# Two blocks of fp32 layers on one core: four weight buffers of each kind, gated products ended token tile by token tile, later transposes in the feed-forwards

## The chip, the cores and the metric

One core of a Trainium2 chip runs the whole program. The metric is device time in microseconds (us), the median of several executions. The core has a matrix engine (TensorE, PE in the rows), a vector engine (VectorE, DVE), a scalar engine (ScalarE, ACT), GpSimd (POOL) and a queue engine (SyncE, SP) that here only issues transfers.

## The reference

The first block has two layers of feed-forward, mixer, feed-forward. The second has an even layer (Hyena convolution with window attention, then an MLP, both for 256 tokens and 256 context tokens) and an odd one (retention, then an MLP for the tokens alone), each modulated by rows that come from a small conditioning product (ada). Width is 1024, batch 1, all in fp32.

```python
x = x + 0.5 * swiglu(rms_norm(x), w_gate, w_up, w_down)       # 2816 wide
x = x + merged @ w_out                                        # mixer
x = x + 0.5 * swiglu(rms_norm(x), ...)
...
x = x + g_a * y_l                                             # even, odd mixer
x = x + g_m * sq_relu_mlp(modulate(rms_norm_2(x)), w1, w2)    # 4096 wide
ctx = ctx + cg_a * y_c
ctx = ctx + cg_m * sq_relu_mlp(modulate(rms_norm_2(ctx)), w1, w2)
...
return rms_norm_2(x, final_g)
```

## The kernel before, in words

Each fp32 product is made of three matmuls on split operands: high by high, high by low and low by high. Weights come in tiles of two k tiles by 512 columns (512 KB). `wload` (L237) issues the transfer into wraw on SP, rounds it to whi on ScalarE (L251) and subtracts to get wlo on VectorE (L252). A short table, `ENG`, sets for the first tiles after a gated output product which subtraction goes to POOL instead (one after a product of two token tiles, two after one of four). Buffers of wraw, whi and wlo are 4, 3 and 3, taken in turn in `wtile`; the feed-forwards add 3, 1 and 1 and the mixers of the first block 0, 1 and 1.

`gemm` (L261) keeps a token tile of 128 still and moves 512 weight columns through, for 2 or 4 token tiles (L291 to L293). It takes the weight tiles in order; for the last group, if `skew` says so, it takes each token tile to its end before the next. `gemm_t` (L299) keeps weights still and moves tokens (L333 to L335), 256 or 512 columns.

`ffn` (L456) walks the 2816 columns in six chunks. Each chunk is a gate product, an up product, av (L473, VectorE), eight transposes of av on TensorE (L477), and their split into ahi and alo (L480); then `residual` (L445) does the down product. `out_gated` (L1323) is the output product of both mixers of the second block and of the MLPs: when a token tile ends, `add_gated` (L1053, L1054) adds it to x or ctx, and the norm of the next stage begins: `prep_mod` (L399) transposes x (L410), takes row statistics (L353, L359, L343, POOL for the power, L345), spreads the scales with a ones product (L424 from junk, L423; rb, L425), and then scales (L429) and splits (hA L432, hB L433) the operand of the next stage. Between them are three handovers: even mixer to MLP 0, MLP 0 to odd mixer, odd mixer to MLP 1. In the first block kdup (L565) is an operand of the mixer's attention, transposed at L670.

A tile scheduler sets the order on each engine from the program's order and its priorities; ada work (L987, L999, L1003) is put in between as background, a step per weight load. Each engine takes its instructions strictly in that order. The token-tile end reads

```python
elif last:
    order = [(k, t) for t in range(nt) for k in part]
```

Of the kernel before, what the change touches and what calls it, by code (L numbers as in the profile page):

```python
# [11 lines left out]
F32 = mybir.dt.float32  # L12
# [20 lines left out]

ENG = {2: [0, 1], 4: [0, 1, 1]}
# [65 lines left out]
class Net:  # L100
# [30 lines left out]
    def setup(self):  # L131
# [3 lines left out]
        self.eng = []  # L135
# [90 lines left out]
    def wtile(self, name, shape):  # L226

        own = {"wraw": 4, "whi": 3, "wlo": 3}[name]
# [8 lines left out]
    def wload(self, src, k0, nk, c0, cn):  # L237
# [8 lines left out]
        with self.tc.high_priority(120 if self.loads <= 2 else 0):  # L246
            e = self.eng.pop(0) if self.eng else 0
            if e & 2:
                nc.gpsimd.tensor_copy(hi[sl], raw[sl])
            else:  # L250
                nc.scalar.copy(hi[sl], raw[sl])  # L251
            (nc.gpsimd if e & 1 else nc.vector).tensor_sub(lo[sl], raw[sl], hi[sl].bitcast(F32))  # L252
# [8 lines left out]
    def gemm(self, lhs, nk, src, c0, cn, nt, k_base=0, mid=None, done=None, skew=(False, False), turn=0):  # L261
# [7 lines left out]
        group = 2 if cn > 256 else 1  # L269
        i = 0  # L270
        while i < len(plan):
            if mid and i == min(2, len(plan) - 1):
                mid()
            n = 1
            if nt == 4 and i == 0 and skew[0] or skew[1] and i == len(plan) - group:
                n = group
# [5 lines left out]
            if i == 0 and skew[0] and nt == 4:  # L282
                order = [(k, t) for ts in ((0, 1), (2, 3)) for k in part for t in ts]
# [4 lines left out]
            for (kt, wh, wl), t in order:  # L288
                h, l = lhs(kt + k_base, t)
# [9 lines left out]
    def gemm_t(self, hT, nk, src, c0, cn, tok, skew=False, whole=False):  # L299
# [10 lines left out]
        group = 2 if cn > 256 else 1  # L310
        i = 0
        while i < len(plan):
# [86 lines left out]
    def prep_mod(self, x, m, tok, kind, xA):  # L399

        nc = self.nc
        ss = self.sm.tile([128, 2, 4], F32, name="ssm")
        seen = []

        def piece(c0, cn):
            k0 = c0 // 128
            ps = [self.tp.tile([128, 2, 256], F32, name="tp") for _ in range(cn // 256)]
            for t in range(2):
                for i in range(cn // 128):
                    nc.tensor.transpose(ps[i // 2][:, i % 2, t * 128:t * 128 + 128], x[:, t, (k0 + i) * 128:(k0 + i) * 128 + 128], self.ident)  # L410
            for i in range(cn // 128):
                nc.scalar.activation(xA[:, k0 + i], ps[i // 2][:, i % 2], AF.Copy, scale=m[:, tok, kind + 1, k0 + i:k0 + i + 1])
            self.row_stats(x, ss, len(seen), c0=c0, cn=cn)
            seen.append(c0)

        rb = self.act.tile([128, 1, 256], F32, name="rb", bufs=2)
# [1206 lines left out]
```

## Time and profile before

| what | value |
|---|---|
| median of 3 runs | 2446.25 us (2445.13 to 2447.65) |
| profiled execution, its own time | 2448.74 us |
| its span | 2447.0 us |
| TensorE busy | 2379.9 us (97%) |
| VectorE busy | 1542.1 us (63%) |
| ScalarE, POOL busy | 1107.5 us (45%), 145.1 us (6%) |
| DMA | 405.85 MB, 166 GB/s mean |

The span is the profiled part of one execution; the rest of the execution's own time lies around it. Matmuls overlap, so a busy TensorE is not one at its peak. PEclk in a window is the clock granted to TensorE, 1.00 for the full one. A wait is put down to what ended it last.

### The profile page before, as it was taken

How to read it: one execution, taken by the hardware profiler on the slowest of the kernel's cores; microseconds unless marked ns; L12 is line 12 of the kernel's file. 1: busy time of each engine (PE TensorE's matmuls, PEld its weight loads, DVE VectorE, ACT ScalarE, POOL GpSimd, SP SyncE). 2: the span in 40 equal slices, each digit the busy share in tenths (PEclk: the TensorE clock that was granted, in tenths of full speed). 3: DMA queues.
4: the chain of work that ended last, by engine and by line, in shares of the span. 5: the costliest groups of instructions: out<-in, count | busy, mean ns of one | idle time of the engine just before them, and what ended most of it. 6: DMA issues, size and time to landing. Idle time of an engine off the chain costs nothing. (4 is left out here: it accounts for less than half of the span.)

```text
span 2447.0 us, 31298 instructions
## 1 busy us (share of the span) xinstructions
PE 2379.9 (97%) x11941; PEld 1924.1 (79%) x11941; DVE 1542.1 (63%) x2237; ACT 1107.5 (45%) x1715; POOL 145.1 (6%) x175
## 2 busy tenths in 40 slices
PE   9999999999999999999999999999999999999998
PEld 7887777778788867778887767788887888887996
DVE  5775677756767557685855765555534654565665
ACT  5444664544444456554543434331424433334543
POOL 2000100110000000000000001000001110110000
PEclk9999999999999999999999999999999999999999
DMA  8775536856777554586642122645432433344664
GB/s 273 249 254 183 165 121 196 265 168 211 241 215 225 174 164 140 163 277 186 218 146 90 53 86 69 193 167 170 141 99 86 140 103 104 112 129 138 198 182 137
DMA packets 212350, 405.85 MB, mean 166 GB/s; under 512 B 14830, under 2 KB 48365, under 8 KB 211688
## 3 DMA queue, kind: packets, MB, share of 16 engines
q1 hardware_dynamic: 207416, 391.77, 50.8%
q0 software_dynamic: 3776, 9.38, 1.2%
q10 hardware_dynamic: 1008, 2.70, 0.3%
q8 instruction: 94, 1.54, 0.3%
q14 instruction: 56, 0.46, 0.1%
HBM read 401.48 MB, written 4.67 MB: 166 GB/s over the span
## 5 line engine op out<-in xcount | busy, mean ns | idle before, releaser
L252 DVE TENSOR_TENSOR wlo<-wraw,whi 128x1024 fp32r<-128x1024 f32 (+1 forms) x617 | 750.8, 1221 | 588.1 <-ACT whi L251 585.9
L251 ACT CAST whi<-wraw 128x1024 fp32r<-128x1024 f32 (+1 forms) x622 | 649.1, 1046 | 952.5 <-PE acc L293 707.7
L291 PE MATMUL acc<-whi,hA 128*128 128x512 f32 (+1 forms) x1472 | 561.0, 381 | 1.8 <-ACT hA L378 0.8
L292 PE MATMUL acc<-wlo,hA 128*128 128x512 f32 (+1 forms) x1472 | 556.9, 378 | 0.3 <-DVE wlo L252 0.3
L293 PE MATMUL acc<-whi,hA 128*128 128x512 f32 (+2 forms) x1152 | 432.5, 375 | 1.4 <-DVE hA L379 1.4
L291 PEld LDWEIGHTS acc<-whi,hA 128*128 128x128 f32 x1472 | 278.1, 189 | 61.0 <-issue 8.6
L292 PEld LDWEIGHTS acc<-wlo,hA 128*128 128x128 f32 x1472 | 278.3, 189 | 49.1 <-DVE wlo L252 1.7
L291 PE MATMUL acc<-whi,ahi 128*128 128x512 f32 x736 | 288.5, 392 | 0.0
L293 PE MATMUL acc<-whi,alo 128*128 128x512 f32 x736 | 286.8, 390 | 0.0
L292 PE MATMUL acc<-wlo,ahi 128*128 128x512 f32 x736 | 286.7, 390 | 0.0
L333 PE MATMUL acc<-hA,whi 128*128 128x512 f32 (+1 forms) x752 | 259.5, 345 | 6.4 <-ACT rl L1385 3.4
L334 PE MATMUL acc<-hA,wlo 128*128 128x512 f32 (+1 forms) x752 | 259.2, 345 | 2.4 <-POOL wlo L252 2.4
L335 PE MATMUL acc<-hB,whi 128*128 128x512 f32 (+1 forms) x752 | 257.8, 344 | 0.0
L293 PEld LDWEIGHTS acc<-whi,hA 128*128 128x128 f32 x1152 | 218.0, 189 | 40.4 <-DVE hA L379 2.0
L333 PEld LDWEIGHTS acc<-hA,whi 128*128 128x128 f32 x752 | 144.8, 193 | 25.2 <-ACT rl L1385 3.8
L291 PEld LDWEIGHTS acc<-whi,ahi 128*128 128x128 f32 x736 | 138.2, 188 | 30.2 <-issue 2.3
L334 PEld LDWEIGHTS acc<-hA,wlo 128*128 128x128 f32 x752 | 145.1, 193 | 21.4 <-issue 3.4
L293 PEld LDWEIGHTS acc<-whi,alo 128*128 128x128 f32 x736 | 138.2, 188 | 29.3 <-issue 0.4
L292 PEld LDWEIGHTS acc<-wlo,ahi 128*128 128x128 f32 x736 | 138.2, 188 | 28.1 <-issue 0.2
L335 PEld LDWEIGHTS acc<-hB,whi 128*128 128x128 f32 x752 | 144.6, 193 | 17.2 <-issue 1.4
L999 DVE SCALAR_TENSOR_TENSOR hB<-hB,cT 128x1024 f32<-128x1024 f32 x112 | 141.0, 1279 | 22.1 <-DMA hB<-in_ada_w_dram 21.8
L293 PE MATMUL acc<-whi,hB 128*128 128x512 f32 (+1 forms) x320 | 121.5, 382 | 2.5 <-DVE hB L433 2.4
(422 smaller groups left out, 2544.2 us busy)
## 6 DMA issues: line engine op xcount, KB each, us to landing
wraw<-in_mlp_w_dram SPq DMA_DIRECT2D x128, 512.0 KB, 3.8
wraw<-in_ffn_w_gate_dram SPq DMA_DIRECT2D x88, 512.0 KB, 4.2
wraw<-in_ffn_w_up_dram SPq DMA_DIRECT2D x88, 512.0 KB, 4.6
wraw<-in_ffn_w_down_dram SPq DMA_DIRECT2D x88, 512.0 KB, 4.0
wraw<-in_w_in_dram SPq DMA_DIRECT2D x84, 512.0 KB, 3.7
hB<-in_ada_w_dram SPq DMA_DIRECT2D x64, 512.0 KB, 4.9
wraw<-in_od_w_in_dram SPq DMA_DIRECT2D x64, 512.0 KB, 3.7
xA<-in_ada_w_dram SPq DMA_DIRECT2D x32, 512.0 KB, 4.4
```

The source lines that it names most:

```text
L251: nc.scalar.copy(hi[sl], raw[sl])
L252: (nc.gpsimd if e & 1 else nc.vector).tensor_sub(lo[sl], raw[sl], hi[sl].bitcast(F32))
L291: nc.tensor.matmul(o, h, wh, start=kt == first, stop=False)
L292: nc.tensor.matmul(o, h, wl, start=False, stop=False)
L293: nc.tensor.matmul(o, l, wh, start=False, stop=kt == end)
L333: nc.tensor.matmul(o, wh[:, cs], xh[:, kt, ts], start=st, stop=False, skip_group_check=skew_or_pair)
L334: nc.tensor.matmul(o, wl[:, cs], xh[:, kt, ts], start=False, stop=False, skip_group_check=skew_or_pair)
L335: nc.tensor.matmul(o, wh[:, cs], xl[:, kt, ts], start=False, stop=en, skip_group_check=skew_or_pair)
L999: nc.vector.scalar_tensor_tensor(acc[tok], raw, c, acc[tok], op0=ALU.mult, op1=ALU.add)
```

## The change

All three kinds of weight buffer are four; the descriptor scratch of POOL's transfers is set to 8192 bytes. `ENG` is gone: every split is on ScalarE and VectorE. In `gemm` and `gemm_t` the group at an end or a beginning is four weight tiles (eight k tiles) where it was two, so that a gated product ends token tile by token tile over its last 24 matmuls each, and the next stage's first product takes eight k tiles of the context (or first) tokens before it turns to the others; a `mid` hook is placed by a count of products. The transposes of av move from behind the up product to 24 matmuls into the next gate product (or the down product). The odd mixer's output norm is by token tile, the first chunk of MLP 1 uses `gemm` with eight transposes of its squares, and the last gated sums get a higher priority.

```diff
@@ -30,8 +30,6 @@
 CB = 4
-ENG = {2: [0, 1], 4: [0, 1, 1]}
@@ -132,7 +130,6 @@
         self.loads = 0
-        self.eng = []
         self.more_weights()
@@ -225,7 +222,7 @@
-        own = {"wraw": 4, "whi": 3, "wlo": 3}[name]
+        own = 4
         more = self.more.get(name, 0)
@@ -244,12 +241,8 @@
         with self.tc.high_priority(120 if self.loads <= 2 else 0):
-            e = self.eng.pop(0) if self.eng else 0
-            if e & 2:
-                nc.gpsimd.tensor_copy(hi[sl], raw[sl])
-            else:
-                nc.scalar.copy(hi[sl], raw[sl])
-            (nc.gpsimd if e & 1 else nc.vector).tensor_sub(lo[sl], raw[sl], hi[sl].bitcast(F32))
+            nc.scalar.copy(hi[sl], raw[sl])
+            nc.vector.tensor_sub(lo[sl], raw[sl], hi[sl].bitcast(F32))
         self.tick()
@@ -266,26 +259,28 @@
         first, end = plan[0][0], sum(plan[-1]) - 1
-        group = 2 if cn > 256 else 1
-        i = 0
+        group = 4 if cn > 256 else 2
+        i = done_k = 0
+        wait = 6 if skew[1] and len(plan) == group else min(4, nk - 2) * nt
         while i < len(plan):
-            if mid and i == min(2, len(plan) - 1):
-                mid()
             n = 1
-            if nt == 4 and i == 0 and skew[0] or skew[1] and i == len(plan) - group:
+            if i == 0 and skew[0] or skew[1] and i == len(plan) - group:
                 n = group
...
             last = i + n == len(plan)
-            if i == 0 and skew[0] and nt == 4:
-                order = [(k, t) for ts in ((0, 1), (2, 3)) for k in part for t in ts]
+            if i == 0 and skew[0]:
+                order = [(k, t) for ts in (((0, 1), (2, 3)) if nt == 4 else ((0,), (1,))) for k in part for t in ts]
             elif last:
...
             for (kt, wh, wl), t in order:
+                if mid and done_k == wait:
+                    mid()
+                done_k += 1
                 h, l = lhs(kt + k_base, t)
@@ -307,7 +302,7 @@
         plan = self.tiles(src, nk, c0, cn)
-        group = 2 if cn > 256 else 1
+        group = 4 if cn > 256 else 2
         i = 0
@@ -319,7 +314,8 @@
                 hf = nt // 2
-                order = [(k, c, slice(q * hf, q * hf + hf)) for q in range(2) for k in part for c in cols]
+                order = [(k, c, slice(q * hf, q * hf + hf)) for q in range(2)
+                         for ks in [part[j:j + 2] for j in range(0, len(part), 2)] for c in cols for k in ks]
             elif last:
@@ -396,37 +392,40 @@
-    def prep_mod(self, x, m, tok, kind, xA):
-        nc = self.nc
-        ss = self.sm.tile([128, 2, 4], F32, name="ssm")
+    def prep_mod(self, x, m, tok, kind, xA, nt=2):
+        nc = self.nc
+        n = 128 * nt
+        ss = self.sm.tile([128, nt, 4], F32, name="ssm")
         seen = []
...
@@ -434,7 +433,7 @@
         def finish(hi, lo, col0, run=True):
-            steps = [scales] + [lambda kp=kp: part(hi, lo, slice(col0, col0 + 256), kp) for kp in range(4)]
+            steps = [scales] + [lambda kp=kp: part(hi, lo, slice(col0, col0 + n), kp) for kp in range(4)]
             if not run:
@@ -442,14 +441,14 @@
-    def residual(self, x, lhs, nk, src, f, nxt=None):
+    def residual(self, x, lhs, nk, src, f, nxt=None, first=None):
         nc = self.nc
...
-            self.gemm(lhs, nk, src, h * 512, 512, 2, done=done, mid=(lambda: nxt[0](0, 512)) if nxt and h == 1 else None)
+            self.gemm(lhs, nk, src, h * 512, 512, 2, done=done, mid=(lambda: nxt[0](0, 512)) if nxt and h == 1 else None if h else first)
         if nxt:
@@ -461,10 +460,25 @@
             alo = fp.tile([128, 22, 256], F32R, name="alo", bufs=1)
+            def turn(c0, cn, t, av):
+                nb = cn // 128
+                ps = self.tp.tile([128, 4, 128], F32, name="tp")
+                for b in range(nb):
+                    nc.tensor.transpose(ps[:, b], av[:, b * 128:b * 128 + 128], self.ident)
+                sl = (slice(None), slice(c0 // 128, c0 // 128 + nb), slice(t * 128, t * 128 + 128))
+                nc.scalar.copy(ahi[sl], ps[:, :nb])
+                nc.vector.tensor_sub(alo[sl], ps[:, :nb], ahi[sl].bitcast(F32))
+            late = []
+            def turn_late():
+                while late:
+                    turn(*late.pop(0))
             for c0 in range(0, F1, 512):
                 cn = min(512, F1 - c0)
-                nb = cn // 128
-                g = self.gemm(lhs, 8, wg, c0, cn, 2)
+                g = self.gemm(lhs, 8, wg, c0, cn, 2, mid=turn_late)
                 u = self.gemm(lhs, 8, wu, c0, cn, 2)
@@ -472,17 +486,12 @@
                                                    op0=ALU.mult, op1=ALU.mult)
-                    ps = self.tp.tile([128, 4, 128], F32, name="tp")
-                    for b in range(nb):
-                        nc.tensor.transpose(ps[:, b], av[:, b * 128:b * 128 + 128], self.ident)
-                    sl = (slice(None), slice(c0 // 128, c0 // 128 + nb), slice(t * 128, t * 128 + 128))
-                    nc.scalar.copy(ahi[sl], ps[:, :nb])
-                    nc.vector.tensor_sub(alo[sl], ps[:, :nb], ahi[sl].bitcast(F32))
+                    late.append((c0, cn, t, av))
                 if hook:
...
             self.residual(x, lambda kt, t: (ahi[:, kt, t * 128:t * 128 + 128], alo[:, kt, t * 128:t * 128 + 128]),
-                          22, wd, 0.5, nxt)
+                          22, wd, 0.5, nxt, first=turn_late)
             self.drain_fill()
@@ -1339,19 +1349,18 @@
                     xs, row = (ctx[:, t], rows[1]) if t < 2 else (x[:, t - 2], rows[0])
-                self.add_gated(xs[:, c0:c0 + cn], acc[:, :cn], row[:, c0:c0 + cn])
+                with self.tc.high_priority(400 if last else 0):
+                    self.add_gated(xs[:, c0:c0 + cn], acc[:, :cn], row[:, c0:c0 + cn])
                 if after:
                     after(t, c0, cn)
-                if pres and c0 and t % 2:
-                    p = pres[t // 2]
+                if pres and c0 and (nt == 2 or t % 2):
+                    p = pres[t if nt == 2 else t // 2]
                     p[0](c0, cn)
                     if last:
-                        p[1](*hT, 256 if nt == 2 else 256 * (t // 2))
+                        p[1](*hT, 256 + 128 * t if nt == 2 else 256 * (t // 2))
...
                       skew=(False, bool(last or after and c0)), turn=0 if c0 else turn)
-        if pres:
-            self.eng = list(ENG[nt])
         return hT
@@ -1371,11 +1380,32 @@
             rows = [self.mod_row(mp, i, tok, 5, "gm%d" % tok) for tok in range(2 if ctx is not None else 1)]
+            turns = []
             for part in range(F2 // 512 // nchunk):
...
                     lo = mp.tile([128, 4, ntok], F32R, name="alo", bufs=nchunk)
+                    parts.append((hi, lo))
+                    if ctx is None and part == 0 and ch == 0:
+                        xlhs = lambda kt, t: tuple(h[:, kt, 256 + t * 128:384 + t * 128] for h in hT)
+                        acc = self.gemm(xlhs, 8, w1, 0, 512, nt, skew=(True, False))
+                        for t in range(nt):
+                            sq = mp.tile([128, 2, 256], F32, name="sq", bufs=2)
+                            rl = mp.tile([128, 2, 256], F32, name="rl", bufs=2)
+                            flat = lambda v: v.rearrange("p a n -> p (a n)")
+                            nc.scalar.activation(flat(rl), acc[t], AF.Relu)
+                            nc.vector.tensor_mul(sq, rl, rl)
+                            def turn(t=t, sq=sq, hi=hi, lo=lo):
+                                ps = self.tp.tile([128, 4, 128], F32, name="tp")
+                                for c in range(4):
+                                    nc.tensor.transpose(ps[:, c], sq[:, c // 2, c % 2 * 128:c % 2 * 128 + 128], self.ident)
+                                ts = slice(t * 128, t * 128 + 128)
+                                self.put_split(hi[:, :, ts], lo[:, :, ts], ps)
+                            turns.append(turn)
+                        continue
                     banks = self.gemm_t(hT, 8, w1, (part * nchunk + ch) * 512, 512, toks,
@@ -1386,7 +1416,8 @@
                         self.put_split(hi[:, c], lo[:, c], sq)
-                    parts.append((hi, lo))
+                    while turns:
+                        turns.pop(0)()
                 lhs = lambda kt, t: tuple(p[:, kt % 4, t * 128:t * 128 + 128] for p in parts[kt // 4])
@@ -1503,8 +1534,8 @@
             xA = op.tile([128, 8, 256], F32, name="Vh")
-            pre = self.prep_mod(x, m, 0, 3, xA)
-            return self.out_gated(x, None, ylhs, 16, a["od_w_out_2"][0], [ga], [pre], new_hT)
+            pres = [self.prep_mod(x[:, t:t + 1], m, 0, 3, xA[:, :, t * 128:t * 128 + 128], 1) for t in range(2)]
+            return self.out_gated(x, None, ylhs, 16, a["od_w_out_2"][0], [ga], pres, new_hT)
@@ -1609,7 +1640,7 @@
 def kernel(**inputs):
-    nc = bacc.Bacc("TRN2", target_bir_lowering=False, num_devices=1)
+    nc = bacc.Bacc("TRN2", target_bir_lowering=False, num_devices=1, dynamic_dma_scratch_size=8192)
     arrays, args = {}, {}
```

How the order moves, at three places. First VectorE at the first turn of layer 0's second feed-forward: L999 and L1008 are ada work, av the gated product, alo the low half of its transpose. Before:

```order
L999 SCALAR_TENSOR_TENSOR hB<-hB,cT 128x1024
L252 TENSOR_TENSOR wlo<-wraw,whi 128x1024
L999 SCALAR_TENSOR_TENSOR hB<-hB,cT 128x1024
L252 TENSOR_TENSOR wlo<-wraw,whi 128x1024
L473 SCALAR_TENSOR_TENSOR av<-acc,rs,sg 128x512 x2
L999 SCALAR_TENSOR_TENSOR hB<-hB,cT 128x1024
L480 TENSOR_TENSOR alo<-tp,ahi 128x4x128 x2
L252 TENSOR_TENSOR wlo<-wraw,whi 128x1024
L999 SCALAR_TENSOR_TENSOR hB<-hB,cT 128x1024
```

and with the change:

```order
L245 TENSOR_TENSOR wlo<-wraw,whi 128x1024 x4
L1008 SCALAR_TENSOR_TENSOR hB<-hB,cT 128x1024 x2
L487 SCALAR_TENSOR_TENSOR av<-acc,rs,sg 128x512 x2
L245 TENSOR_TENSOR wlo<-wraw,whi 128x1024 x2
L1008 SCALAR_TENSOR_TENSOR hB<-hB,cT 128x1024
L245 TENSOR_TENSOR wlo<-wraw,whi 128x1024
L1008 SCALAR_TENSOR_TENSOR hB<-hB,cT 128x1024
L245 TENSOR_TENSOR wlo<-wraw,whi 128x1024
L471 TENSOR_TENSOR alo<-tp,ahi 128x4x128 x2
```

Four weight splits and two ada operations now stand between av and alo, where one ada operation stood; on TensorE the transposes of av between them are one row of eight, 18 to 24 weight matmuls further on than before.

Second VectorE from even mixer to MLP 0: b holds the transposed operand (one for the context, one for the tokens), modT the modulation. Before:

```order
L423 TENSOR_SCALAR junk<-k_ident,rs 128x128 x2
L429 TENSOR_TENSOR b_12294<-b_12294,rb 128x512 x3
L433 SCALAR_TENSOR_TENSOR hB<-b_12294,modT_9316,hA 128x256 x6
L429 TENSOR_TENSOR b_12294<-b_12294,rb 128x512
L1053 TENSOR_TENSOR junk<-acc,b_12291 128x512 x2
L433 SCALAR_TENSOR_TENSOR hB<-b_12294,modT_9316,hA 128x256 x2
L1054 TENSOR_TENSOR x<-x,junk 128x512 x2
```

and with the change:

```order
L422 TENSOR_SCALAR junk<-k_ident,rs 128x128 x2
L428 TENSOR_TENSOR b_12294<-b_12294,rb 128x512 x3
L432 SCALAR_TENSOR_TENSOR hB<-b_12294,modT_9302,hA 128x256 x3
L1062 TENSOR_TENSOR junk<-acc,b_12291 128x512
L432 SCALAR_TENSOR_TENSOR hB<-b_12294,modT_9302,hA 128x256
L1063 TENSOR_TENSOR x<-x,junk 128x512
L432 SCALAR_TENSOR_TENSOR hB<-b_12294,modT_9302,hA 128x256 x2
L428 TENSOR_TENSOR b_12294<-b_12294,rb 128x512
L245 TENSOR_TENSOR wlo<-wraw,whi 128x1024
L432 SCALAR_TENSOR_TENSOR hB<-b_12294,modT_9302,hA 128x256 x2
L245 TENSOR_TENSOR wlo<-wraw,whi 128x1024
L1062 TENSOR_TENSOR junk<-acc,b_12291 128x512
```

Splits of MLP 0's weights now stand between the context's split (hB) and the gated sums of the last token tile, which are taken one by one. On TensorE there are 38 512-wide and 36 256-wide matmuls between the context's ones products and the tokens', where there were 14 and 35.

Third VectorE from odd mixer to MLP 1: Vh is the transposed operand, kr the gate. Before:

```order
L359 TENSOR_REDUCE s_18063<-ssm 128x2
L343 TENSOR_SCALAR ms<-s_18063 128x2
L423 TENSOR_SCALAR junk<-k_ident,rs 128x128 x2
L429 TENSOR_TENSOR Vh<-Vh,rb 128x512 x3
L433 SCALAR_TENSOR_TENSOR hB<-Vh,modT_14393,hA 128x256 x6
L429 TENSOR_TENSOR Vh<-Vh,rb 128x512
```

and with the change:

```order
L355 TENSOR_REDUCE s_18083<-ssm 128x1
L339 TENSOR_SCALAR ms<-s_18083 128x1
L422 TENSOR_SCALAR junk<-k_ident,rs 128x128
L245 TENSOR_TENSOR wlo<-wraw,whi 128x1024
L428 TENSOR_TENSOR Vh<-Vh,rb 128x2x128
L1062 TENSOR_TENSOR junk<-acc,kr 128x512
L428 TENSOR_TENSOR Vh<-Vh,rb 128x2x128
L1063 TENSOR_TENSOR x<-x,junk 128x512
L432 SCALAR_TENSOR_TENSOR hB<-Vh,modT_14441,hA 128x128 x4
```

Token tile 0's norm now stands before the gated sum of token tile 1. On TensorE, 55 matmuls of the output product now follow the transposes of x's first half where the ones products did; token 1's last transposes stand two matmuls into MLP 1's first product.

## Rows read from the trace of the kernel before

**Rows 1.** Page, first line: span and instructions.

```profile
span 2447.0 us, 31298 instructions
```

**Rows 2.** TensorE's waits, whole span: waited for, us in total, times, longest.

```profile
PE tp L477 <- DVE av L473: 10.5, 7, 4.1
...
PE tp L670 <- DVE kdup L565: 4.5, 2, 2.3
```

**Rows 3.** The same list, 1494 to 1552 us, even mixer to MLP 0.

```profile
PE acc L333 <- ACT rl L1385: 3.4, 1, 3.4
PE acc L334 <- POOL wlo L252: 2.4, 1, 2.4
PE acc L333 <- ACT hA L432: 1.3, 1, 1.3
PE tp L424 <- DVE junk L423: 1.0, 2, 0.6
```

**Rows 4.** The same list, 1875 to 1900 us, MLP 0 to odd mixer.

```profile
PE acc L293 <- DVE hB L433: 1.8, 1, 1.8
PE tp L410 <- DVE x L1054: 1.2, 1, 1.2
PE tp L424 <- DVE junk L423: 0.8, 1, 0.8
```

**Rows 5.** The same list, 2240 to 2260 us, odd mixer to MLP 1.

```profile
PE tp L410 <- DVE x L1054: 2.3, 1, 2.3
PE tp L424 <- DVE junk L423: 2.0, 1, 2.0
PE acc L333 <- ACT hA L432: 1.7, 1, 1.7
```

**Rows 6.** Windows: from:to us; PE, PEld, DVE, ACT, POOL busy; PEclk, DMA, GB/s.

```profile
456.00:470.00 14.00, 9.93 (x41) 7.91 (x41) 12.84 (x13) 5.13 (x6) 0.00 (x0) 0.88 0.75 254
1097.00:1108.00 11.00, 9.12 (x38) 7.23 (x38) 6.63 (x12) 4.10 (x5) 0.00 (x0) 0.84 0.65 203
1495.00:1505.00 10.00, 10.00 (x56) 8.40 (x54) 3.88 (x5) 4.69 (x11) 0.00 (x0) 1.00 0.31 99
1515.00:1525.00 10.00, 7.53 (x48) 7.15 (x49) 7.22 (x11) 4.17 (x12) 4.00 (x3) 0.83 0.37 107
1540.00:1555.00 15.00, 11.65 (x40) 9.05 (x39) 10.67 (x13) 4.95 (x8) 0.00 (x0) 0.77 0.70 233
2255.00:2260.00 5.00, 5.00 (x26) 4.87 (x25) 2.82 (x7) 1.33 (x4) 0.00 (x0) 0.54 0.00 0
2262.00:2272.00 10.00, 10.00 (x85) 10.00 (x84) 6.73 (x10) 5.86 (x8) 0.60 (x1) 1.00 0.73 210
2400.00:2424.00 24.00, 24.00 (x108) 19.87 (x106) 14.20 (x16) 10.84 (x13) 0.00 (x0) 1.00 0.61 192
```

**Rows 7.** Timeline of TensorE, first turn of layer 0's second feed-forward: start, us.

```profile
463.29 0.66 PE L477 MATMUL tp<-k_ident,av 128*128 128x128 f32 x4 [4.07 <-DVE av L473]
```

**Rows 8.** Timeline of VectorE at the same turn.

```profile
461.36 1.22 DVE L252 TENSOR_TENSOR wlo<-wraw,whi 128x1024 fp32r<-128x1024 f32 x1
462.49 1.40 DVE L473 SCALAR_TENSOR_TENSOR av<-acc,rs,sg 128x512 f32<-128x512 f32 x2
```

**Rows 9.** Timeline of VectorE, even mixer to MLP 0.

```profile
1508.71 1.90 DVE L429 TENSOR_TENSOR b<-b,rb 128x512 f32<-128x512 f32 x3 [1.07 <-ACT rb L425]
1510.53 2.46 DVE L433 SCALAR_TENSOR_TENSOR hB<-b,modT,hA 128x256 fp32r<-128x256 f32 x6
...
1514.70 3.88 DVE L433 SCALAR_TENSOR_TENSOR hB<-b,modT,hA 128x256 fp32r<-128x256 f32 x2
```

**Rows 10.** Timeline of POOL in the same stretch.

```profile
1512.97 5.33 POOL L252 TENSOR_TENSOR wlo<-wraw,whi 128x1024 fp32r<-128x1024 f32 x2 [5.85 <-ACT whi L251]
```

**Rows 11.** Timeline of TensorE, second eight of sixteen transposes in a row.

```profile
1497.16 1.04 PE L410 MATMUL tp<-k_ident,x 128*128 128x128 f32 x8
```

**Rows 12.** DMA issues of POOL: KB each, median us to landing.

```profile
gm<-mods POOLq DMA_DIRECT2D x3, 512.0 KB, 7.6
```

More of the change, by code (lines that the diff above doesn't have):

```diff
@@ L406, in piece @@
             k0 = c0 // 128
-            ps = [self.tp.tile([128, 2, 256], F32, name="tp") for _ in range(cn // 256)]
-            for t in range(2):
+            per = 4 // nt
+            ps = [self.tp.tile([128, per, n], F32, name="tp") for _ in range(cn // 128 // per)]
+            for t in range(nt):
                 for i in range(cn // 128):
-                    nc.tensor.transpose(ps[i // 2][:, i % 2, t * 128:t * 128 + 128], x[:, t, (k0 + i) * 128:(k0 + i) * 128 + 128], self.ident)
+                    nc.tensor.transpose(ps[i // per][:, i % per, t * 128:t * 128 + 128], x[:, t, (k0 + i) * 128:(k0 + i) * 128 + 128], self.ident)
             for i in range(cn // 128):
-                nc.scalar.activation(xA[:, k0 + i], ps[i // 2][:, i % 2], AF.Copy, scale=m[:, tok, kind + 1, k0 + i:k0 + i + 1])
-            self.row_stats(x, ss, len(seen), c0=c0, cn=cn)
+                nc.scalar.activation(xA[:, k0 + i], ps[i // per][:, i % per], AF.Copy, scale=m[:, tok, kind + 1, k0 + i:k0 + i + 1])
+            self.row_stats(x, ss, len(seen), nt, c0=c0, cn=cn)
             seen.append(c0)
-        rb = self.act.tile([128, 1, 256], F32, name="rb", bufs=2)
+        rb = self.act.tile([128, 1, n], F32, name="rb", bufs=2)
         def scales():
             r = self.row_rstd(ss[:, :, :len(seen)])
-            dg = self.act.tile([128, 2, 128], F32, name="junk", bufs=2)
-            ps = self.tp.tile([128, 2, 128], F32, name="tp")
-            for t in range(2):
+            dg = self.act.tile([128, nt, 128], F32, name="junk", bufs=2)
+            ps = self.tp.tile([128, nt, 128], F32, name="tp")
+            for t in range(nt):
                 nc.vector.tensor_scalar(dg[:, t], self.ident, r[:, t:t + 1], None, op0=ALU.mult)
@@ L428, in part @@
             ks = slice(2 * kp, 2 * kp + 2)
-            nc.vector.tensor_mul(xA[:, ks], xA[:, ks], rb.to_broadcast([128, 2, 256]))
+            nc.vector.tensor_mul(xA[:, ks], xA[:, ks], rb.to_broadcast([128, 2, n]))
             for kt in (2 * kp, 2 * kp + 1):
@@ L1378, in mlp @@
                     lo = mp.tile([128, 4, ntok], F32R, name="alo", bufs=nchunk)
+                    parts.append((hi, lo))
+                    if ctx is None and part == 0 and ch == 0:
+                        xlhs = lambda kt, t: tuple(h[:, kt, 256 + t * 128:384 + t * 128] for h in hT)
+                        acc = self.gemm(xlhs, 8, w1, 0, 512, nt, skew=(True, False))
+                        for t in range(nt):
+                            sq = mp.tile([128, 2, 256], F32, name="sq", bufs=2)
[11 more added lines that the diff above has]
+                        continue
                     banks = self.gemm_t(hT, 8, w1, (part * nchunk + ch) * 512, 512, toks,
```

## Prediction

> **What bounds the kernel now.** I read the page first: one core, a span of 2447.0 us [rows 1], with TensorE busy nearly all the time, so only three things can shorten it: matmul time, time in which TensorE waits, and time at its lower clock. No product of the model goes away. The list of TensorE's waits comes next; the reader is to see there that one tile, the transposes of the feed-forward product av, waited 10.5 us in 7 places [rows 2]. Then the same list for three stretches, the handovers from one gated output product to the next stage: even mixer to MLP 0 [rows 3], MLP 0 to the odd mixer [rows 4], odd mixer to MLP 1 [rows 5]: 8.1, 3.8 and 6.0 us. Then the windows by stage [rows 6], for the granted clock behind each stall (the full level is 2.4 GHz, 1.00 in the row; the lower, 1.2 GHz, is half). Last the timelines of VectorE and POOL, to see why an operand was late.
>
> **Sum against which execution.** The durations come from the profiled run, 2448.74 us by its own timer; the median of the three timed runs is 2446.25, so 2.5 come off at the end.
>
> **Paces.** 24.00 us of 512-wide products hold 106 weight loads, 0.2264 us each; 10.00 us of 256-wide ones hold 84, 0.119 each [rows 6].
>
> **Feed-forward turn (24 of them, six column chunks in each of four feed-forwards).** Before, the transposes of av stand right behind the up product. TensorE waited up to 4.1 us for av [rows 7], since VectorE had a weight split and modulation work (1.22 us the split) ahead of av in its order [rows 8]. Now the eight transposes come 24 weight matmuls into the next product: 24 x 0.2264 = 5.4 us of cover, over the longest wait of 4.1. So all 10.5 us should go. The clock dips behind two of these waits go with them: 14.00 us at 0.88 lost 1.7, 11.00 at 0.84 lost 1.8 [rows 6]. **Gone: 14.0.** What is late next is alo, which VectorE makes from the transposes; it is read only in the down product, and the last chunk's k tiles come last there. VectorE's order has about five tiles split ahead at that point, some 60 matmuls or 13.6 us of work for TensorE, so two alo operations of about 0.64 cost nothing; without that cover they would cost 1.3 a turn (a rival below).
>
> **Even mixer to MLP 0.** Four waits, 8.1 us [rows 3]. Their causes: the weight splits sat on POOL, where two took 5.33 us, and in that time two hB operations on VectorE took 3.88 us, while six shortly before took 2.46, 0.41 each [rows 9, 10]. With the split table gone, POOL has none. The 3.4 us for rl came from MLP 0's second chunk: VectorE's order had a modulation operation that waited for its ada transfer, and the squares of rl were queued behind it. That transfer was behind weight loads on SP's queue, which waited for a free wraw. Now eight weight loads are followed by three ada loads at once and the four weight copies are split earlier, so I take it as gone. The clock rows give 10.00 x 0.17 = 1.7 and 15.00 x 0.23 = 3.5 [rows 6]. **Gone: 8.1 + 5.2 = 13.3.** What comes back: the context's ones products still stand five matmuls behind its last transposes, so the wait for junk, 1.0, stays. And VectorE now does, between the context's and the tokens' ones products, four row scalings and four gated operations at 0.63, eight hB at 0.41 and four splits at 1.22: 2.5 + 2.5 + 3.3 + 4.9 = 13.2 us, against 38 x 0.2264 + 36 x 0.119 = 12.9 us and eight transposes on TensorE. That is a tie, so waits must be expected; bounds are 0 (transposes and slack cover it) and 7.1 (the rest of the old waits). I take 2.6, as VectorE's lead is small but not negative. **Stays: 3.6.** The first product of MLP 0 is now 192 matmuls of 256 columns (22.8 us) in place of 96 and 48 of 512 (11.4 + 10.9): **0.5 more**.
>
> **MLP 0 to odd mixer.** Three waits of 3.8 [rows 4], no clock loss. One output token now gives 24 matmuls, 5.4 us, where it gave 2.7, to the chain behind the other. Gone 3.8; between 0 and 3.8 returns; I take 1.0 (the same five-matmul ones product as above, whose wait was 0.8). **2.8 gained.**
>
> **Odd mixer to MLP 1.** Waits of 2.3, 2.0 and 1.7, 6.0 together [rows 5], all on one chain: the gated sum of both tokens, transposes, statistics, ones product, scaling, hA. The clock was 0.54 for 5.00 us behind it: 2.3 [rows 6]. **Gone: 8.3.** Now token 0's norm runs while token 1's 24 products run. What is left: token 1's transposes have two matmuls (0.45) ahead of them against two gated operations of 0.63: 0.8. Token 0's hA has four matmuls (0.9) behind the ones product where there were none and the wait was 1.7: 0.8. VectorE has four splits of 1.22 between its two token norms: 1.5, an estimate between 0 and 4.9. **Stays: 3.1** (bounds 0 and 6.0). The first chunk of MLP 1 by `gemm` costs 48 x 0.2264 + 8 transposes, at most 1.04 [rows 11], for 96 x 0.119: **0.5 more**. The Trainium skill ("TensorE: Matmul & The Clock Gate", Part 4: PE-mode transpose) gives about 275 ns for a transpose in a kernel's context; by it the eight would be 2.2 us and this term 1.7; the row decides for 1.04.
>
> **What gets worse.** In both mixers of the first block more weight tiles make the scheduler put kdup's transposes eight weight matmuls (1.8 us) earlier and another group four (0.9) earlier. kdup was already late by 4.5 us in two places [rows 2], as its VectorE operations don't move with it. Bounds 0 and 2 x 2.7 = 5.4; I take **2.8**, half, since VectorE also splits less at that point.
>
> **Buffers.** Four tiles of each kind own room in all stages; the smaller scratch for POOL's descriptors pays for it. POOL's transfers are the same as before; one that a stage needs, gm, lands in 7.6 us [rows 12], but is issued as MLP 0 begins and read only in its output product. No row shows a full ring. I take 0; from below 0, from above one landing at a stage edge, 7.6. **End of the kernel:** the gated sum's priority moves nothing there that a row prices; 0.
>
> **Sum.** Gone 14.0 + 13.3 + 3.8 + 8.3 = 39.4. Back or new 3.6 + 0.5 + 1.0 + 3.1 + 0.5 + 2.8 = 11.5. Net 27.9: 2448.74 becomes 2420.8, and the median 2446.25 becomes **2418**.
>
> **Rivals.**
> R1, the handovers only move their waits. VectorE is the limit there (the tie above), so all 17.9 us of waits and their 7.5 of clock come back and only the turns gain: 14.0 - 1.0 - 2.8 = 10.2, **2436**. For: the tie. Against: a third of these waits came from POOL's splits and the ada transfer, which go.
> R2, everything goes and nothing comes back: 39.4, **2407**. For: 5.4 us of cover per token against waits of at most 3.4. Against: the short distances to the ones products.
> R3, nothing gained: the turns wait for alo instead, 24 x 1.3 = 31 lost against 28, so **2449**. It needs the five-tile lead on VectorE to be gone at every turn, and the order shows that lead in all of them.
> R4, slower. The eight transposes of a turn now stand in one block, where a matmul stood between two fours. If TensorE's clock falls at each block, as it did behind two turns for 1.8 us, 24 blocks lose 43: **2461**. It ends above no change by more than a measurement can tell (0.2%, 4.9 us) from 19 of the 24 on. Against: 16 transposes in a row, eight of them in [rows 11], ran in a window of clock 1.00 [rows 6]; the falls stood behind waits. The Trainium skill's same section says that transposes do not count as TensorE activity for the clock; by that rule R4 would be the likely case, and the trace does not agree for blocks this short.
>
> **How the numbers follow.** Forecast 0.66, R1 0.14, R2 0.07, R3 0.07, R4 0.06. The range from 2407 (R2) to 2435 takes in the forecast's bounds (mixers 5.4, one landing of 7.6) and about half of R1: 0.66 + 0.07 + 0.07 = 0.80. Faster by over 0.2%: forecast, R1, R2: 0.87. Within: R3, 0.07. Slower: R4, 0.06.
>
> **What would show it.** Right: no wait for av in TensorE's list; in the three handovers 2 to 9 us of waits in all; clock 0.95 or more there; no split on POOL; kdup's wait at 6 to 8 us. Wrong: waits for alo in a down product; a clock under 0.9 behind the av transposes (R4); hB or junk waits of 15 us and more at the handovers (R1); weight waits (whi, wlo) in mid-stage, which would mean that the four-tile first groups starve the product.

## The result, and the profile after

The change runs in **2410.57 us** (median of four runs, 2406.18 to 2413.85) where the kernel before ran in 2446.95 (four runs beside it, 2445.13 to 2453.3): a ratio of 0.9845, 95% interval 0.9824 to 0.9865, 36.4 us or 1.5% faster. Run again beside other kernels it took 2409.01 against 2447.33, ratio 0.9837 (0.9823 to 0.9852). The forecast was 2418, with a range from 2407 to 2435: the direction and the range held, and the gain of 28 was 8 us too small.

The profiled execution took 2406.18 us, its span is 2404.4. TensorE's list of waits for the whole span, as before (waited for: us in total, times, longest). Lines of code have moved: L468 and L487 are the transposes of av and av, L679 and L574 those of kdup, L423 and L422 the ones product and junk, L831 and L838 another operand of the mixers:

```profile
PE tp L838 <- DVE big L831: 4.1, 2, 2.0
PE tp L423 <- DVE junk L422: 3.3, 6, 0.9
PE tp L468 <- DVE av L487: 2.5, 3, 1.1
PE tp L679 <- DVE kdup L574: 2.5, 2, 1.5
...
PE acc L286 <- ACT hA L431: 1.8, 2, 1.5
...
PE acc L329 <- ACT rl L1415: 0.3, 1, 0.3
```

The waits for av went from 10.5 us to 2.5 [rows 2], those for kdup from 4.5 to 2.5, where 6 to 8 was expected. The three handovers, in the same list by stretch (1462 to 1530, 1812 to 1863 and 2182 to 2235 us, the three parts between the dots):

```profile
PE tp L423 <- DVE junk L422: 1.3, 2, 0.7
PE acc L329 <- ACT rl L1415: 0.3, 1, 0.3
...
PE tp L423 <- DVE junk L422: 0.5, 1, 0.5
...
PE acc L286 <- ACT hA L431: 1.8, 2, 1.5
PE tp L423 <- DVE junk L422: 0.7, 2, 0.4
PE acc L287 <- DVE wlo L245: 0.3, 1, 0.3
```

8.1, 3.8 and 6.0 us [rows 3 to 5] became 1.6, 0.5 and 2.8. Nothing waits for wlo on POOL, and rl is down from 3.4 to 0.3. The clock came back too: the granted clock is 1.00 in each of the three stretches. Span and mean granted clock of the kernel before, then of the change:

```profile
core 0: 2447.0 us, clock 0.992
```

```profile
core 0: 2404.4 us, clock 0.998
```

The clock's loss is 2447.0 x 0.008 = 20 us before and 2404.4 x 0.002 = 5 after: some 15 of the 42.6 us between the two profiled executions (14 with the clocks' further digits) is clock. That part differs from run to run: the four runs of the change had mean clocks of 0.998, 0.997, 0.997 and 0.995 and took 2406.18, 2410.05, 2411.10 and 2413.85 us.

To see where time went, I summed over TensorE's instructions what each interval from start to start exceeds the usual one of its shape (0.227 us for 512 columns, 0.120 for 256, the kernel's median for the rest). This **lost time** holds waits and clock alike. By stage, in us, for the profiled execution of each kernel ("even entry" is the way into the even mixer, the three columns after it are the handovers, "rest" is all else):

| kernel | feed-forwards | mixers | even entry | even to MLP 0 | MLP 0 to odd | odd to MLP 1 | rest | sum |
|---|---|---|---|---|---|---|---|---|
| before | 41.7 | 35.0 | 3.5 | 13.9 | 5.9 | 9.7 | 31.8 | 141.6 |
| the change | 22.4 | 34.6 | 1.2 | 2.8 | 1.4 | 4.5 | 31.8 | 98.7 |
| the change again | 27.8 | 32.6 | 1.2 | 3.1 | 1.4 | 4.5 | 31.9 | 102.4 |
| late transposes alone | 30.0 | 35.2 | 3.3 | 14.6 | 5.9 | 9.1 | 32.3 | 130.4 |
| four buffers alone | 42.6 | 36.5 | 1.7 | 11.7 | 4.6 | 9.7 | 31.8 | 138.6 |
| these two | 26.7 | 35.7 | 1.7 | 13.3 | 3.7 | 10.3 | 31.9 | 123.2 |
| change, turn at once | 38.3 | 35.8 | 1.2 | 3.8 | 1.4 | 4.5 | 31.9 | 116.8 |
| change, splits on POOL | 23.6 | 32.4 | 1.2 | 8.3 | 5.8 | 7.3 | 31.8 | 110.3 |
| change, groups of two | 24.8 | 34.0 | 1.8 | 13.2 | 4.8 | 7.8 | 31.8 | 118.1 |
| change, norm whole | 27.9 | 34.6 | 1.2 | 2.9 | 1.4 | 9.5 | 31.8 | 109.3 |
| change, MLP 1 by gemm_t | 22.7 | 32.6 | 1.2 | 3.0 | 1.4 | 12.7 | 31.8 | 105.4 |

Of the 42.9 us, 19.3 come from the feed-forwards, 11.1, 4.5 and 5.2 from the handovers, 2.3 from the entry of the even mixer and 0.4 from the first block's mixers. The two profiles of the change itself differ by 5.4 us in the feed-forwards, by 2.0 in the mixers and by 0.3 at most in the handovers; so a difference of some 5 us in the first column, or of 2 in the second, says nothing by itself.

### The profile page after: what moved, and what is told of

Its sections match the earlier page's. It is cut to its first block, busy times and chain, and to the rows that moved or that the text cites. A ratio compares the mean times of both kernels' runs of the same rounds, so it can differ in the third digit from the quotient of the medians.

```text
span 2404.4 us, 31410 instructions
## 1 busy us (share of the span) xinstructions
PE 2362.7 (98%) x11949; PEld 1917.4 (80%) x11949; DVE 1535.9 (64%) x2256; ACT 1109.8 (46%) x1734; POOL 131.3 (5%) x171
## 4 chain that ended last, share of the span: by engine, by line
PE 86%; DVE 5%; ACT 2%; DMA 2%; POOL 2%; issue 2%; POOLq 0%; SPq 0%; DVEq 0%; ACTq 0%
PE acc L286 20%; PE acc L287 20%; PE acc L288 20%; PE acc L330 5%; PE acc L329 5%; PE acc L331 5%; DVE wlo L245 2%; DMA hB<-in_ada_w_dram 1%; PE tp L1496 1%; PE tp L1215 1%; PE tp L468 1%; PE acc L1298 1%; PE tp L1316 1%; PE tp L1250 1%; PE tp L751 1%
## 5 line engine op out<-in xcount | busy, mean ns | idle before, releaser
L286 PE MATMUL acc<-whi,hA 128*128 128x512 f32 (+1 forms) x1488 | 566.7, 381 | 2.8 <-ACT hA L431 1.8
L329 PE MATMUL acc<-hA,whi 128*128 128x512 f32 (+1 forms) x736 | 250.6, 341 | 0.3 <-ACT rl L1415 0.3
L330 PE MATMUL acc<-hA,wlo 128*128 128x512 f32 (+1 forms) x736 | 250.3, 340 | 0.0
L331 PE MATMUL acc<-hB,whi 128*128 128x512 f32 (+1 forms) x736 | 249.5, 339 | 0.0
L287 PEld LDWEIGHTS acc<-wlo,ahi 128*128 128x128 f32 x736 | 138.2, 188 | 27.9
L330 PEld LDWEIGHTS acc<-hA,wlo 128*128 128x128 f32 x736 | 139.6, 190 | 17.9 <-issue 3.4
L329 PEld LDWEIGHTS acc<-hA,whi 128*128 128x128 f32 x736 | 139.6, 190 | 17.7 <-issue 1.7
L1008 DVE SCALAR_TENSOR_TENSOR hB<-hB,cT 128x1024 f32<-128x1024 f32 x112 | 141.4, 1280 | 17.9 <-DMA hB<-in_ada_w_dram 17.8
L331 PEld LDWEIGHTS acc<-hB,whi 128*128 128x128 f32 x736 | 139.6, 190 | 16.1 <-issue 1.4
L288 PE MATMUL acc<-whi,hB 128*128 128x512 f32 (+1 forms) x336 | 128.1, 381 | 0.0
```

The source lines that it names most:

```text
L286: nc.tensor.matmul(o, h, wh, start=kt == first, stop=False)
L287: nc.tensor.matmul(o, h, wl, start=False, stop=False)
L288: nc.tensor.matmul(o, l, wh, start=False, stop=kt == end)
L329: nc.tensor.matmul(o, wh[:, cs], xh[:, kt, ts], start=st, stop=False, skip_group_check=skew_or_pair)
L330: nc.tensor.matmul(o, wl[:, cs], xh[:, kt, ts], start=False, stop=False, skip_group_check=skew_or_pair)
L331: nc.tensor.matmul(o, wh[:, cs], xl[:, kt, ts], start=False, stop=en, skip_group_check=skew_or_pair)
```

## The experiments

**Late transposes alone**, on the kernel before (this and the other edits are shown in short):

```diff
-                    ps = self.tp.tile(...)          # transposes at once
+                    late.append((c0, cn, t, av))    # and turn_late() 24 matmuls into the next product
```

> The kernel before with the late transposes of av alone (24 weight matmuls into the next product, also in the down product); buffers, table of splits, groups and norms as before. Theory A (the turn's cover alone takes the av waits away): the waits for av fall from 10.5 us to under 3, their clock dips go, the time falls by 14 to 19 us to 2428 to 2433; the handovers keep their waits of 8.1, 3.8 and 6.0 us. Theory B (the cover works only with four low and high buffers, which give VectorE its lead): waits for alo or wlo appear in the feed-forwards and less than 7 us are gained, over 2440.

Measured 2436.05 against 2446.97, ratio 0.9958 (0.9944 to 0.9973): 10 us, under what theory A gave and over theory B. The waits of this kernel (L472 and L491 are av; L373 waits for x, L453, at the end of a feed-forward; L336 waits for MLP 0's rl, L1398):

```profile
PE tp L683 <- DVE kdup L578: 5.3, 2, 2.7
PE acc L336 <- ACT rl L1398: 4.6, 2, 4.3
...
PE tp L373 <- DVE x L453: 3.9, 3, 2.3
...
PE tp L472 <- DVE av L491: 1.9, 2, 1.1
```

av is down to 1.9, so the cover (the matmuls put between av and its transposes) works without more buffers. But x at the feed-forwards' ends is at 3.9 us, against 2.1 in the list of before (L370 there, with the mixers' operand, L829, for later):

```profile
PE tp L829 <- DVE big L822: 2.6, 2, 1.6
...
PE tp L370 <- DVE x L450: 2.1, 3, 1.1
```

The last chunk's turn and its alo now fall into the down product, which might delay x; that is not shown, since this wait was 1.1 and 2.3 us in the two profiles of the change, which has the same late turn.

**Four buffers alone**, on the kernel before:

```diff
-        own = {"wraw": 4, "whi": 3, "wlo": 3}[name]
+        own = 4
...
-num_devices=1)
+num_devices=1, dynamic_dma_scratch_size=8192)
```

> The kernel before with four buffers of each kind and the smaller descriptor scratch alone. Theory A (buffers pay only in the mixers' kdup, whose two reductions now stand behind each other with no weight split between): kdup wait 2 to 3 us instead of 4.5, av wait and handovers within 3 us of before, time 2441 to 2447. Theory D (the buffers carry the handovers): handover waits under 9 us in all instead of 17.9, time under 2436.

Measured 2440.26 against 2446.97, ratio 0.9974 (0.9963 to 0.9986): 6 us, just beyond theory A's range, far from D's. The waits (L477, L473 av; L670, L565 kdup; L829, L822 the other operand):

```profile
PE tp L477 <- DVE av L473: 12.0, 8, 3.6
...
PE tp L829 <- DVE big L822: 4.1, 2, 2.0
...
PE tp L670 <- DVE kdup L565: 2.0, 2, 1.0
```

kdup fell as theory A said, av did not, and handover waits stayed in the main. Its profiled execution had a mean clock of 0.989 (2443.8 x 0.011 = 27 us lost, against 20 before), so its row in the table shows the gain only in part. Of the table's columns the even mixer's entry (3.5 to 1.7), even mixer to MLP 0 (13.9 to 11.7) and MLP 0 to odd mixer (5.9 to 4.6) are lower; with the late transposes added the second is back at 13.3. So where the 6 us come from is shown only in part. The kdup gain can be followed on VectorE. Before, then with the change (timeline, start and duration; hs is the reduction ahead of kdup):

```profile
216.10 0.28 DVE L525 TENSOR_REDUCE hs<-junk 128x2 f32<-128x128 f32 x1
217.40 1.22 DVE L252 TENSOR_TENSOR wlo<-wraw,whi 128x1024 fp32r<-128x1024 f32 x1 [1.02 <-ACT whi L251]
218.55 0.28 DVE L525 TENSOR_REDUCE hs<-junk 128x2 f32<-128x128 f32 x1
...
220.15 0.90 DVE L565 TENSOR_TENSOR kdup<-nat,hr 128x128 f32<-128x128 f32 x4 [1.12 <-POOL hr L528]
```

```profile
213.60 2.46 DVE L245 TENSOR_TENSOR wlo<-wraw,whi 128x1024 fp32r<-128x1024 f32 x2 [3.29 <-ACT whi L244]
215.98 0.28 DVE L534 TENSOR_REDUCE hs<-junk 128x2 f32<-128x128 f32 x1
216.69 0.29 DVE L534 TENSOR_REDUCE hs<-junk 128x2 f32<-128x128 f32 x1 [0.43 <-ACT junk L533]
...
218.31 0.90 DVE L574 TENSOR_TENSOR kdup<-nat,hr 128x128 f32<-128x128 f32 x4 [1.13 <-POOL hr L537]
```

Before, a weight split stood between the two reductions. With another buffer it is done earlier, the second reduction ends 1.9 us earlier, and the transposes, which the order put 1.8 us earlier, wait less, not more.

**Both together**, on the kernel before:

> The kernel before with both the late transposes of av and four buffers of each kind (smaller descriptor scratch); splits on POOL, groups, norms as before. Alone the two gained 10 and 6 us. Theory A (they add): 2428 to 2432, and the feed-forwards' ends keep the waits of late transposes alone (x 2.3 and hA 1.6 us in layer 1's second feed-forward). Theory J (the late transposes put work at the feed-forward's end which only more split-ahead absorbs): those waits fall under 1 us each and 20 to 24 us are gained, 2422 to 2427.

Measured 2428.24 against 2447.33, ratio 0.9915 (0.9898 to 0.9932), 19 us by medians, 21 by the ratio. That is the low end of theory A's range, and x still waited 2.5 us (1.8 at the longest), as theory A said; hA's wait at a feed-forward's end was gone, as theory J said. The two add up, with at most a few us from working together.

**The changed kernel with the turn at once**:

```diff
-                    late.append((c0, cn, t, av))
+                    turn(c0, cn, t, av)
```

> The changed kernel with the transposes of av right behind the up product again; all else as changed. Theory A: the av waits come back, 14 to 19 us slower than the change, 2425 to 2430, handovers as in the change. Theory C (four buffers of each kind already take the wait away, since splits are made earlier and leave VectorE free when the up product ends): av waits under 4 us and less than 6 us slower than the change, under 2417.

Measured 2426.01, ratio 0.992 (0.9894 to 0.9945) to before: 15 us slower than the change, as theory A said (the differences here are to 2410.57; to its second median, 2409.01, they are 1.6 more). Handovers as in the change. The wait is back in full:

```profile
PE tp L468 <- DVE av L487: 12.1, 9, 4.6
```

**The turn's transposes twice**, the change with 16 in a row:

```diff
-                for b in range(nb):
+                for b in range(2 * nb):
+                    b %= nb
```

> The changed kernel with each of the 176 transposes of av done twice into the same place: blocks of 16 instead of 8. Theory A (a row of transposes costs its own time and no clock): 176 x 0.109 = 19 us slower than the change, 2428 to 2432, mean granted clock 0.995 or more, no low-clock stretch behind the blocks. Theory E (a block without products lowers the clock): 24 stretches at the lower clock, 1.7 us lost at each, 40 us more on top, 2465 to 2475, mean clock about 0.98.

Measured 2428.62, 18 us over the change, mean clock 0.997. The timeline of TensorE at one turn, then a window with the six blocks of one feed-forward, five of 16 transposes and one of 8 (from:to us; PE, PEld, DVE, ACT, POOL busy; PEclk, DMA share, GB/s):

```profile
473.64 1.91 PE L469 MATMUL tp<-k_ident,av 128*128 128x128 f32 x16
```

```profile
450.00:600.00 150.00, 150.00 (x742) 120.51 (x742) 97.54 (x113) 75.50 (x87) 10.19 (x9) 1.00 0.64 205
```

Sixteen transposes took 1.91 us, 0.119 each, at the full clock. Theory E falls, and with it the rival that ended slower: blocks of this length cost their time and no clock. One turn of this run, the last of the first feed-forward, did have a low-clock stretch behind it; it had waited 3.2 us for av. The Trainium skill ("TensorE: Matmul & The Clock Gate", Part 4: PE-mode transpose) gives some 275 ns for a bf16 transpose in one kernel's context and says that transposes don't engage the full clock. The trace agrees on the time of a single one, from its start to the end that the profile models for it (272 ns, the median of the 176 in the change, in fp32). But in a row they overlap and cost 119 ns each, so the 275 can't be multiplied by a count, and the clock held.

**Splits back on POOL**, in the change (five of them, after three products):

```diff
+            self.eng = list({2: [0, 1], 4: [0, 1, 1]}[nt])      # after out_gated with pres
...
-            nc.vector.tensor_sub(lo[sl], raw[sl], hi[sl].bitcast(F32))
+            (nc.gpsimd if e & 1 else nc.vector).tensor_sub(lo[sl], raw[sl], hi[sl].bitcast(F32))
```

> The changed kernel with the table of splits back: after each gated output product the second (of two token tiles) or second and third (of four) low-half subtractions of the next stage on POOL; all else as changed. Theory A (POOL's splits slow VectorE's hB, 1.94 us against 0.41 beside them, and come late themselves): waits for wlo or hB return at the handovers, 3 to 8 us slower than the change, 2413 to 2419. Theory F (with eight k tiles of the context first there is cover enough, where the split runs matters no more, and VectorE is even freer): within 2 us of the change.

Measured 2421.58, ratio 0.9893 (0.9876 to 0.9909): 11 us slower than the change, more than theory A gave. TensorE's longest waits are not for wlo or hB, as theory A had it, but for x, which stands behind hB on VectorE:

```profile
PE tp L411 <- DVE x L1065: 7.2, 2, 3.8
```

The longer of the two is from even mixer to MLP 0; timelines of POOL, VectorE and TensorE (L1065 is the gated sum of x, L411 its transposes):

```profile
1486.78 5.30 POOL L247 TENSOR_TENSOR wlo<-wraw,whi 128x1024 fp32r<-128x1024 f32 x2 [8.25 <-ACT whi L246]
```

```profile
1487.25 5.11 DVE L434 SCALAR_TENSOR_TENSOR hB<-b,modT,hA 128x256 fp32r<-128x256 f32 x2
1492.28 0.68 DVE L1064 TENSOR_TENSOR junk<-acc,b 128x512 f32<-128x512 f32 x1
1493.00 0.69 DVE L1065 TENSOR_TENSOR x<-x,junk 128x512 f32<-128x512 f32 x1
```

```profile
1493.74 1.11 PE L411 MATMUL tp<-k_ident,x 128*128 128x128 f32 x4 [3.79 <-DVE x L1065]
```

The same two hB operations in the change:

```profile
1487.89 0.88 DVE L432 SCALAR_TENSOR_TENSOR hB<-b,modT,hA 128x256 fp32r<-128x256 f32 x2
```

5.11 us against 0.88: VectorE stood nearly still while POOL subtracted, and the sum of x, queued behind hB, came 3.79 us late for TensorE, with a low-clock stretch behind it. The trace of before had shown this price already (3.88 us for two, [rows 9, 10]). The Trainium skill ("SBUF — State Buffer", Who interferes with whom) says that a VectorE instruction with two SBUF inputs contends with a GpSimd instruction that reads SBUF; the trace agrees: hB reads two, and its time went up by 4.23 us beside a POOL span of 5.30.

**Groups of two weight tiles again**, in the change:

```diff
-        group = 4 if cn > 256 else 2
+        group = 2 if cn > 256 else 1
```

> The changed kernel with end and first groups of two weight tiles again (12 matmuls for each token tile at the end, four k tiles of the context first); buffers, splits, norm by token tile and late turns as changed. Theory A (the cover of 24 matmuls per token tile carries the handovers): from even mixer to MLP 0 the waits and slow clock go from 2.8 us in the change back to 8 to 13, MLP 0 to odd mixer from 1.4 to 3 to 6, odd mixer to MLP 1 from 4.5 to 6 to 9; 9 to 18 us slower than the change, 2420 to 2428. Theory G (buffers and splits off POOL carry them): under 5 us slower.

Measured 2423.31, ratio 0.99 (0.9885 to 0.9915): 13 us slower than the change. Theory A holds, at all three places of the table (13.2, 4.8, 7.8); the first is just over its range. The waits of this run:

```profile
PE tp L423 <- DVE junk L422: 6.0, 4, 2.3
...
PE acc L329 <- ACT rl L1415: 3.2, 1, 3.2
...
PE tp L409 <- DVE x L1063: 1.8, 1, 1.8
PE acc L329 <- ACT hA L431: 1.7, 1, 1.7
```

rl is back at 3.2 us, and it was 4.1 with late transposes and buffers. So the groups of four removed it, not the buffers or the splits' place. The edit changes the groups at the beginning and at the end of a product together; that it is the first group, by the order of its ada loads, is not shown.

**The odd mixer's norm for both token tiles at once**, in the change:

```diff
-                if pres and c0 and (nt == 2 or t % 2):
+                if pres and c0 and t % 2:
...
-            pres = [self.prep_mod(x[:, t:t + 1], ..., 1) for t in range(2)]
+            pre = self.prep_mod(x, m, 0, 3, xA)
```

> The changed kernel with the odd mixer's output norm for both token tiles at once (MLP 1's first chunk still by token tile). Theory A (the norm by token tile is what shortens the handover from odd mixer to MLP 1): its waits go from 2.8 us back to 5 to 6 with the lower clock behind them, lost time there 8 to 11 us instead of 4.5, 3.5 to 6.5 us slower, 2414 to 2417. Rival H (ending token tile by token tile is enough): within 1.5 us of the change.

Measured 2417.10, ratio 0.9875 (0.986 to 0.989): 6.5 us over the change, lost time there 9.5 against 4.5, as theory A said.

**MLP 1's first chunk by gemm_t**, in the change:

```diff
-                    if ctx is None and part == 0 and ch == 0:
+                    if False:
```

> The changed kernel with MLP 1's first chunk by gemm_t again (weights still, both token tiles moved together), norm by token tile kept. Theory A (token tile 0 alone can no longer start): TensorE waits for the whole chain of token tile 1, waits of 4 to 7 us at this handover in place of 2.8 with the lower clock behind, less 0.5 us of matmul time saved: 2 to 6 us slower, 2412 to 2416. Rival I (the chain of token tile 1 is short, and the saved matmul time counts): 0.5 to 1 us faster than the change.

Measured 2415.32, ratio 0.9866 (0.985 to 0.9882): 5 us over the change, as theory A said. TensorE's waits at this handover are 8.1 us, more than its 4 to 7, the longest for junk:

```profile
PE tp L423 <- DVE junk L422: 5.2, 2, 4.8
PE tp L409 <- DVE x L1063: 1.7, 1, 1.7
PE acc L329 <- ACT hA L431: 1.2, 1, 1.2
```

The windows of this kernel, then of the change, at this handover:

```profile
2205.00:2230.00 25.00, 16.82 (x95) 14.91 (x94) 16.09 (x38) 13.39 (x34) 2.52 (x3) 0.73 0.43 127
```

```profile
2196.00:2221.00 25.00, 22.19 (x98) 16.67 (x97) 16.59 (x37) 13.18 (x34) 1.95 (x2) 1.00 0.48 139
```

**The turn still later**, 36 matmuls into the gate product, and the change once more beside it:

```diff
-                g = self.gemm(lhs, 8, wg, c0, cn, 2, mid=turn_late)
+                g = self.gemm(lhs, 8, wg, c0, cn, 2, mid=turn_late, late=12)
```

> The changed kernel with the transposes of av 36 instead of 24 weight matmuls into the next gate product (24 in the down product as changed). Theory A (2.5 us of av waits are left since the first feed-forward's VectorE is later than 5.4 us at two turns): av waits under 0.7 us, 1 to 3 us faster than the change run beside it. Rival K (what is won there is lost to alo or to the splits behind it): av waits gone, but waits for wlo, whi or x longer by as much, within 1 us.

> The change itself once more, as the neighbour of the two others on the same chip: 2406 to 2414, handovers at 1.6, 0.5 and 2.8 us of waits as in its first profile; the number of low-clock stretches (3.4 us each) may differ from profile to profile, and the time with it.

Side by side: 2408.64 and 2409.01, both with ratio 0.9837. Theory A falls: 2.1 us of av waits are left, all at the last turn of the first feed-forward. The one wait elsewhere, in the third feed-forward (0.5 us in the change's first profile, 0.7 in its second), is gone. In the change's own profile, VectorE and TensorE at that last turn:

```profile
142.87 1.28 DVE L1008 SCALAR_TENSOR_TENSOR hB<-hB,cT 128x1024 f32<-128x1024 f32 x1 [7.07 <-DMA hB<-in_ada_w_dram]
144.07 0.48 DVE L487 SCALAR_TENSOR_TENSOR av<-acc,rs,sg 128x256 f32<-128x256 f32 x1
```

```profile
144.61 0.44 PE L468 MATMUL tp<-k_ident,av 128*128 128x128 f32 x2 [0.91 <-DVE av L487]
```

VectorE stood for 7.07 us at an ada operation whose transfer had not landed; av, next in its order, could not pass, and its second half stood behind a weight split besides. This is the last chunk, whose turn is in the down product, and no number of matmuls in the gate product reaches it. The standstill came with the late turn: all ten profiles that have it show 6.5 to 9.1 us here, the three without it (before, buffers alone, turn at once) 0.6 to 2.2 ahead of this av. Why the transfer lands later was not tested. Rival K is left open: x waited 3.3 us in all against 2.3 beside it, but 1.1 in the change's first profile.

Taken out of the change one at a time, the late turn, POOL without splits, the groups of four, the norm by token tile and MLP 1's first chunk by `gemm` cost 15.4, 11.0, 12.7, 6.5 and 4.8 us, 50 together where the whole change brings 36.4. They act on the same waits, so none of these is a share of the gain. The higher priority of the last gated sums was not taken out by itself.

## Why the prediction was right, and where it was off

- **The turns: right, 14.0 forecast.** Taken out of the change they cost 15.4 us, alone they bring 10 to 11. The step "the transposes come 24 weight matmuls later, so the wait of 4.1 goes" holds at every turn but two: the last of the first feed-forward, 2.0 us in two waits, where VectorE stood at a transfer that lands late with the late turn, and one of the third, 0.5 us. The sign "no wait for av" was therefore missed, by 2.5 us. alo was no new wait in a down product.
- **Even mixer to MLP 0: right in kind, mis-sized.** 3.6 us of waits were to stay; 1.6 did. The ones products waited 1.3 where 1.0 was expected. The tie on VectorE, 2.6, cost nothing that the list shows; 0.3 stayed for rl, which was taken as gone. With no split on POOL hB took 0.44 each, about the time that the sum of 13.2 used, and the 12.9 us of matmuls with eight transposes covered it.
- **MLP 0 to odd mixer: 1.0 to stay, 0.5 did. Odd mixer to MLP 1: 3.1 to stay, 2.8 did**, but otherwise divided: hA 1.8 for 0.8, the ones products 0.7 for nothing, the splits 0.3 for 1.5, and no wait for x, where 0.8 was expected.
- **"What gets worse": wrong sign.** 2.8 us were to be lost in the mixers, since kdup's VectorE operations "don't move with it". They moved: the buffers took the split from between the two reductions. The second group, four matmuls earlier, did wait more (2.6 us to 4.1, with the buffers alone already); together the mixers' lost time fell by 0.4 us, or by 2.4 with the change's second profile.
- **"Buffers: I take 0": wrong.** Alone they bring 6 us. The term priced their room and the smaller scratch, not what an earlier split does on VectorE: kdup, and the even mixer's entry. Whether the smaller scratch has any part in it was not separated.
- **Matmul time**, 0.5 + 0.5 more, can't be told from these numbers: 42.9 us of lost time saved stand against 42.6 of span.
- **The rivals.** R1 fell: the handovers keep 8.7 of their 29.5 us of lost time. With groups of two its part on the handovers would nearly have held, for there they keep 25.8. R2's 2407 lies nearer to 2410.57 than the forecast, but not for its reason: 4.9 us of handover waits came back, and gains that neither had counted made up for them. R3 and R4 fell, R4 by the doubled transposes.
- **The sum.** By lost time the feed-forwards gave 19.3 for 14.0, the handovers 20.8 for 17.7, the mixers 0.4 for a loss of 2.8, the entry 2.3 for nothing: 13.9 more. The profiled pair stands 42.6 apart where the medians stand 36.4, so some 8 of these are in the medians. With the change's second profile the feed-forwards gave 13.9, as forecast, the handovers 20.5, the mixers 2.4 and the entry 2.3: 10.3 more, of which 7.5 are in the mixers and the entry and 2.8 in the handovers. So the terms that failed are those of the mixers and of the buffers, and both erred in the same direction; the handovers had more to give than was counted (29.5 us of lost time, 25.4 "gone" in the sum). How the mixers' part divides between buffers and other moves of the order is not shown.

## What to carry to other kernels

A transpose of a result that VectorE has yet to make belongs as many matmuls behind its producer as VectorE's order can be late, and the cover must be counted at the longest wait, not the mean. When a buffer is added, look at every in-order queue that its producer shares: an earlier split frees the work behind it far from the place for which the buffer was meant. Before work goes to POOL to relieve VectorE, look at what VectorE's operations take beside it.

## What the runs showed of the hardware

Two hB operations on VectorE took 5.11 us beside 5.30 us of subtraction on POOL, 0.88 alone. Transposes in a row cost 0.119 us each (16 in 1.91), and in the window of transposes taken twice the granted clock was 1.00. Low-clock stretches stood behind waits, but not behind each: in the change TensorE waited 2.0 us for the mixers' operand in both layers, and the clock fell behind the second wait and not behind the first (windows as above, PEclk is the third number from the end):

```profile
293.00:298.00 5.00, 4.83 (x42) 4.09 (x43) 4.64 (x13) 3.32 (x7) 0.91 (x1) 1.00 0.59 180
919.00:924.00 5.00, 4.88 (x30) 3.61 (x31) 4.25 (x11) 2.06 (x3) 0.86 (x1) 0.66 0.59 176
```

The four runs of the change, with mean clocks from 0.995 to 0.998, differ by 7.7 us; 0.003 of the span is 7.2.
